# An encoder layer on one core: tokens t and n-t are added and subtracted ahead of the Fourier branch's channel product

## The chip, the cores and the metric

The kernel runs on one core of a Trainium2 chip. The metric is the device time of one execution in microseconds (us), as the median of the runs. The engines are TensorE (PE, its weight loads PEld), VectorE (DVE), ScalarE (ACT), GpSimd (POOL) and SyncE (SP), which issues nearly all DMAs of this kernel.

## What is computed

One layer is applied to two sequences with shared weights, the prompt of 512 tokens and the sample of 1024, 1024 channels each, all in float32. The part that the change touches is the Fourier branch of the mixer:

```python
h = rms_norm(x, g_pre_mix) * (1.0 + sc1) + sh1
u = h @ w_in                      # [xa | ya | xb | ga | gb]
xb = u[..., 2048:2560]
def fourier_mix(x):               # 4 groups of 128 channels
    xg = x.reshape(bsz, s, N_FNET_GROUPS, FNET_GROUP)
    f = jnp.fft.fft2(xg, axes=(1, 3), norm='ortho').real
    return f.reshape(bsz, s, D_FNET)
y_b = fourier_mix(xb) @ w_b_out
merged = sigmoid(ga) * y_a + sigmoid(gb) * y_b
```

Beside it run the RG-LRU branch (`xa`, with two scans in time, times a gelu gate `ya`), the gates `ga` and `gb`, the output projection, and a channel sub-layer with convolutions.

## The kernel before

Every float32 operand is split into two float32r parts, a rounded high part and a low part that is the difference; a product is three matmuls (high by high, high by low, low by high). Activations stand with channels on the partitions and tokens along the columns (`hb["hi"]`, `hb["lo"]`). The split of a weight tile is `prep_unit` / `split`: the high part on DVE (L110) or on ACT (L108), the low part always on DVE (L111).

The program is a list of steps, written out in order by `emit`. A step has a matmul part (`mm`), what follows it (`post`), and maybe a weight unit. Weight units are loaded through three raw buffers and split three steps ahead (`AHEAD`). What `defer` gets runs one or more steps later. Each engine carries out its instructions in the order in which `emit` writes them, and SP issues DMAs in that order too, waiting at each for the buffer that it fills or the tile that it stores. PSUM is a pool of four buffers of two banks (`ps`), SBUF tiles come from a pool of 40 buffers (`big`).

For each sequence the list runs: projections and LRU steps (`mix_heads`, `lru_step`), the Fourier product (`pq_steps`), the gate product (`ya_steps`), the DFT over tokens (`dft_steps`), then the merge. The last step ahead of `pq_steps` is in both sequences the last LRU step. It has four PSUM tiles of products, which ACT reads by tanh (L685), then ACT's exp, tanh and relu (L693 to L697); its DVE work is deferred in three parts: four multiply-adds (s1, L704 and L707), two square roots on ACT (s2, L711, with a table load), and multiplications, scans and a sum (s3, L716 to L724). So this work lies beside the first steps of `pq_steps`.

The channel part of the 2-D DFT is folded into the weights at the start (`fold_in`); the result goes to DRAM (`wxb`, 516 columns: 256 cosine, 4 for the middle frequency, 256 sine). `pq_steps` reads it back in units of 4 channel tiles by 258 columns. For the prompt it makes four token tiles by two halves of the columns; for the sample the later half of the tokens is kept back to front (`mirror`), the product is taken of both halves of the tokens, and the two are added (cosine) or subtracted (sine) behind the product, on DVE, out of PSUM. `dft_steps` then multiplies with cosine and sine tables over 512 token rows in both sequences, four tiles each; for the sample two edge products with the row of the middle token (`pq["row"]`, `odd`) are added for each of three outputs.

The lines of one product are these (the third pass wants the low part of the left operand):

```python
for q, (l, r) in enumerate(((lh, u.hi), (lh, u.lo), (ll, u.hi))):
    self.mmul(
        out, lhsT=l, rhs=r[:, w],
        start=(first and j == 0 and q == 0), stop=(last and j == nk - 1 and q == 2))
```

Of the kernel before, what the change touches and what calls it, by code (L numbers as in the profile page):

```python
# [10 lines left out]
F32 = mybir.dt.float32  # L11
F32R = mybir.dt.float32r
# [5 lines left out]
D = 1024  # L18
# [5 lines left out]
NPQ = 516  # L24
# [7 lines left out]
AHEAD = 3  # L32
LOAD_AHEAD = 5
# [16 lines left out]
class Seq:  # L50
    def __init__(self, name, idx, n, x, y):
        self.name, self.idx, self.n, self.x, self.y = name, idx, n, x, y
        self.nf = 1024 // n
        self.tt = n // 128
        self.chunks = n // 512
        self.groups = KT // self.nf
        self.mirror = n == 1024
        self.pq_tiles = self.tt // 2 if self.mirror else self.tt
# [13 lines left out]
class Enc:  # L72
# [40 lines left out]
    def split_all(self, pairs):  # L113
        """Splits out of PSUM: one engine's reads of a bank before the other's."""
# [112 lines left out]
    def fm_chunks(self, sq, ps, f, mirror=False):  # L227
        """Output columns and the operand's; a mirrored operand has the later half of the tokens back to front."""
        n = sq.n
        cols = [slice(0, 512), slice(n, n // 2, -1) if mirror else slice(512, 1024)]  # L230
        return [(ps[:, f, c * 512:(c + 1) * 512], cols[c]) for c in range(sq.chunks)]

    def fm_steps(self, sq, table, tiles, xh, xl, post, on_act=False, mirror=False):
        box = {}
        steps = []
        for f, m in enumerate(tiles):
            u = Unit(table[m], KT * 128, on_act=on_act)

            def mm(u=u, f=f):
                if f == 0:  # L240
                    box["ps"] = self.ps([128, sq.nf, sq.n])
                self.fm_mm(self.fm_chunks(sq, box["ps"], f, mirror), u, 0, xh(), xl())
# [6 lines left out]
    def setup(self):  # L249
        nc, a = self.nc, self.a  # L250
        self.wxb = self.dram([KT, 128, NPQ], "wxb")
        self.ident = self.const.tile([128, 128], F32, name="ident")
        self.fold = self.const.tile([128, 130], F32, name="fold")
# [67 lines left out]
    def ada_steps(self, job):  # L321
        """One part of the conditioning: a row of its weights per partition, two dot products with each."""
# [65 lines left out]
    def fold_in(self, tiles, out, ks):  # L388
        nc = self.nc
        for k in ks:  # L390
            ps = self.ps([128, 2, 512])
            v = ps[:, :, 0:260].rearrange("p h (g c) -> p h g c", g=2)
            for g in range(4):
                self.mmul(
                    v[:, g // 2, g % 2, :], lhsT=tiles[g][:, k * 128:(k + 1) * 128], rhs=self.fold,
# [3 lines left out]
                out=w[:, 0:256].rearrange("p (h g c) -> p h g c", h=2, g=2), in_=v[:, :, :, 0:64], func=AF.Copy)  # L399
            nc.scalar.activation(  # L400
                out=w[:, 260:516].rearrange("p (h g c) -> p h g c", h=2, g=2), in_=v[:, :, :, 64:128], func=AF.Copy)
            nc.vector.tensor_copy(
                w[:, 256:260].rearrange("p (h g c) -> p h g c", h=2, g=2), v[:, :, :, 128:129])
            out.append(w)

# [26 lines left out]
    def h_steps(self, sq, src, sub, box, quads=False):  # L432
# [15 lines left out]
        def tr(g):  # L448
            def f():
# [7 lines left out]
                mirror = sq.mirror and sub == 0  # L457
                w = n + 2 if mirror else n
                h = self.big([128, sq.nf, w], name="h")
                parts = [(slice(0, 512), slice(0, 512)), (slice(513, 1025), slice(1023, 511, -1))]  # L460
                for i in range(sq.nf):
                    k = g * sq.nf + i
                    for o, src in parts if mirror else [(slice(0, n), slice(0, n))]:
                        nc.scalar.activation(
                            out=h[:, i, o], in_=ps[:, i, src], func=AF.Identity,
                            scale=self.gs[:, sub, sq.idx, k:k + 1], bias=self.mod[:, 3 * sub, sq.idx, k:k + 1])
                if mirror:
# [1072 lines left out]
```

## Time and profile before

| | |
|---|---|
| median of 3 runs | 2117.44 us (2117.34 to 2117.49) |
| the profiled execution, first to last instruction | 2115.4 us |
| PE busy | 2096.1 us, 99% |
| DVE busy | 1424.4 us, 67% |
| ACT busy | 915.9 us, 43% |
| `pq_steps` of the prompt | 194.27 to 217.37 us |
| `pq_steps` of the sample | 692.61 to 738.66 us |

The profiled execution's own time is its span and what lies around it, 2.0 us below the median. Times in the rows further down are microseconds from the start of the span. A matmul's record is longer than the step from one matmul to the next, since matmuls overlap in the engine; so the cost of a matmul is read from a stretch of known count, not from its record. In rows in order of time the columns are: start, duration, engine, line, operation, output <- inputs, shapes, count, and in brackets the idle time ahead of it with what ended it; rows of several instructions are merged, and their duration runs from the first to the last.

### The profile page before, as it was taken

Reading aid. Unit: us, or ns where it says so; the run is one execution under the profiler, and the core shown is the slowest. Engines: PE = TensorE matmul, PEld = TensorE weight load, DVE = VectorE, ACT = ScalarE, POOL = GpSimd, SP = SyncE. Lnnn points to the kernel's source line nnn. Section 1 sums busy time; section 2 is a strip of 40 time slices with the busy share of each in tenths; the row PEclk is TensorE's granted clock in tenths of the full one; section 3 lists DMA queues with packets and bytes.
Section 4 is the critical chain, followed back from the end, with each engine's and each line's share of the span. In section 5 each row is a group of like instructions: output and inputs, shape, how many; then the busy total and the mean of one; then the engine's idle time right before and its main releaser. Section 6 shows DMA issues by size and latency. Waiting matters only on the chain.

```text
span 2115.4 us, 24826 instructions
## 1 busy us (share of the span) xinstructions
PE 2096.1 (99%) x9866; PEld 1721.6 (81%) x9866; DVE 1424.4 (67%) x1815; ACT 915.9 (43%) x1199; POOL 55.0 (3%) x124
## 2 busy tenths in 40 slices
PE   7999999999999999999999999999999999999998
PEld 6888888888888988888888888888888888888887
DVE  5787888667666734655676545649688887875553
ACT  2447355265464422144433335633344444455442
POOL 0000010000000000000100000000000000000000
PEclk9999999999999999999999999999999999999999
DMA  9343474332332413433453224332122222284422
GB/s 350 114 149 130 180 269 162 113 109 85 110 105 65 141 50 108 141 141 135 175 186 112 99 99 156 113 130 90 50 80 80 90 72 82 96 315 163 149 91 109
DMA packets 90803, 274.66 MB, mean 130 GB/s; under 512 B 8736, under 2 KB 26560, under 8 KB 90688
## 3 DMA queue, kind: packets, MB, share of 16 engines
q1 hardware_dynamic: 90688, 273.09, 37.1%
q8 instruction: 77, 1.26, 0.2%
q14 instruction: 38, 0.31, 0.1%
HBM read 234.22 MB, written 38.83 MB: 129 GB/s over the span
## 4 chain that ended last, share of the span: by engine, by line
PE 95%; ACT 2%; DVE 1%; DMA 1%; issue 0%; POOL 0%; SPq 0%; DVEq 0%; POOLq 0%; ACTq 0%
PE ps L200 94%; PE ps L203 1%; DMA x<-in_x_prompt_dram 0%; ACT xn L412 0%; ACT th L685 0%; DVE hl L111 0%; DMA x<-in_x_sample_dram 0%; DVE yb L964 0%; ACT th L695 0%; ACT ea L693 0%; POOL sm L430 0%; DVE th L716 0%; DVE th L721 0%; ACT xn L417 0%; DVE th L719 0%
## 5 line engine op out<-in xcount | busy, mean ns | idle before, releaser
L200 PE MATMUL ps<-hh,hl 128*128 128x512 f32 x2144 | 633.8, 395 | 0.0
L200 PEld LDWEIGHTS ps<-hh,hl 128*128 128x128 f32 x2144 | 403.7, 188 | 95.2 <-DVE hl L111 0.2
L200 PE MATMUL ps<-hl,ah 128*128 128x512 f32 x1440 | 452.2, 395 | 0.0
L200 PE MATMUL ps<-hl,hl 128*128 128x512 f32 (+1 forms) x1264 | 436.2, 378 | 0.0
L111 DVE TENSOR_TENSOR hl<-raw,hl 128x1024 fp32r<-128x1024 f32 (+2 forms) x244 | 293.8, 1206 | 163.3 <-ACT hl L108 160.9
L200 PE MATMUL ps<-hx,wq 128*128 128x512 f32 x1596 | 370.9, 394 | 0.0
L200 PEld LDWEIGHTS ps<-hx,wq 128*128 128x128 f32 x1596 | 299.6, 188 | 71.1 <-DVE wq L1222 0.2
L108 ACT ACTIVATE hl<-raw 128x1024 fp32r<-128x1024 f32 x196 | 205.6, 1054 | 270.8 <-PE ps L200 243.4
L200 PEld LDWEIGHTS ps<-hl,ah 128*128 128x128 f32 x1440 | 269.1, 188 | 61.5
L200 PE MATMUL ps<-hl,al 128*128 128x512 f32 x720 | 283.8, 394 | 0.0
L200 PEld LDWEIGHTS ps<-hl,hl 128*128 128x128 f32 x1264 | 238.3, 189 | 47.5
L200 PEld LDWEIGHTS ps<-hl,al 128*128 128x128 f32 x720 | 135.2, 188 | 31.8
L1318 DVE SCALAR_TENSOR_TENSOR cf<-ps,vec,cf 128x511 f32<-128x511 f32 (+1 forms) x100 | 75.2, 807 | 83.8 <-ACT cf L1310 83.6
L200 PE MATMUL ps<-yh,hl 128*128 128x512 f32 x384 | 111.9, 394 | 0.3 <-DVE hl L111 0.3
L1166 DVE SCALAR_TENSOR_TENSOR cf<-cq,vec,cf 128x1023 f32<-128x1023 f32 x76 | 97.0, 1277 | 0.0
L1221 ACT ACTIVATE wq<-wsum 128x512 fp32r<-128x512 f32 x76 | 46.1, 629 | 117.7 <-DVE wsum L1232 117.7
L200 PEld LDWEIGHTS ps<-yh,hl 128*128 128x128 f32 x384 | 71.5, 188 | 16.9 <-DVE hl L111 0.7
L1310 ACT ACTIVATE cf<-ps,vec 128x512 f32<-128x512 f32 (+1 forms) x50 | 39.1, 826 | 105.9 <-PE ps L200 105.9
L111 DVE TENSOR_TENSOR al<-fq,ah 128x512 fp32r<-128x512 f32 x88 | 57.3, 687 | 32.3 <-PE ps L200 18.4
L738 ACT ACTIVATE sg<-ps 128x1024 f32<-128x1024 f32 x24 | 24.7, 1028 | 118.8 <-PE ps L200 118.7
L200 PE MATMUL ps<-hl,hh 128*128 128x258 f32 x384 | 69.2, 282 | 0.0
L659 DVE SCALAR_TENSOR_TENSOR xc<-ps,vec,xc 128x511 f32<-128x511 f32 (+3 forms) x48 | 46.9, 1012 | 30.1 <-ACT xc L651 29.5
(181 smaller groups left out, 2359.6 us busy)
## 6 DMA issues: line engine op xcount, KB each, us to landing
raw<-in_w_up_dram SPq DMA_DIRECT2D x88, 512.0 KB, 3.5
raw<-in_w_down_dram SPq DMA_DIRECT2D x66, 512.0 KB, 3.5
ada<-in_w_adaT_dram SPq DMA_DIRECT2D x32, 512.0 KB, 4.7
raw<-in_w_o_dram SPq DMA_DIRECT2D x24, 512.0 KB, 3.5
fs<-cf SPq DMA_DIRECT2D x22, 512.0 KB, 2.6
fq<-fs SPq DMA_DIRECT2D x22, 512.0 KB, 5.8
ada<-in_w_ada_dram SPq DMA_DIRECT2D x16, 512.0 KB, 8.9
raw<-in_w_gb_dram SPq DMA_DIRECT2D x16, 512.0 KB, 4.3
```

The source lines that it names most:

```text
L108: nc.scalar.activation(out=hi, in_=src, func=AF.Copy)
L111: nc.vector.tensor_tensor(out=lo, in0=src[:, 0:keep], in1=hi[:, 0:keep].bitcast(F32), op=ALU.subtract)
L200: self.nc.tensor.matmul(*args, **kw)
L203: self.nc.tensor.transpose(*args)
L659: nc.vector.scalar_tensor_tensor(out=xc[:, f, o], in0=ps[:, f, o.start + d:o.stop + d], scalar=w[:, tap:tap + 1], in1=xc[:, f, o], op0=ALU ...
L738: self.nc.scalar.activation(out=t, in_=ps, func=AF.Tanh, scale=0.5)
L1166: nc.vector.scalar_tensor_tensor(out=box[key][:, o], in0=c[:, i], scalar=self.vec[:, V_FW + 3 * m + t:V_FW + 3 * m + t + 1], in1=box[key][ ...
L1221: nc.scalar.activation(out=hi, in_=src, func=AF.Copy)
L1310: nc.scalar.activation(out=acc[:, f, :], in_=ps[:, f, :], func=AF.Identity, scale=w[:, 1:2], bias=self.vec[:, V_FB + m:V_FB + m + 1])
L1318: nc.vector.scalar_tensor_tensor(out=acc[:, f, o], in0=ps[:, f, o.start + d:o.stop + d], scalar=w[:, tap:tap + 1], in1=acc[:, f, o], op0=A ...
```

## The change

The Fourier branch no longer multiplies tokens first and combines them afterwards. Where the modulated activations `h` are made, they are also stored to DRAM (`hrow`: four stores in the lead-in for the prompt, eight in `h_steps` for the sample). `pq_steps` is now four steps for each sequence, over two channel tiles each, with one unit of 2 x 512 columns (split with ACT for the high part). For each step the rows of its channel tiles are read back (`ld`, three steps ahead) and `pair_up` makes sum and difference of token t and token n-t and splits both (two steps ahead). The matmuls of all token tiles accumulate over the four steps: 260 columns with the sums (cosine), 252 with the differences (sine), and a one-row product for token n/2. For this `pq_steps` holds two PSUM buffers for the prompt, three for the sample. The prompt's DFT has two token tiles instead of four and the same edge products as the sample's. The mirrored copies, the additions behind the product, and the `mirror` arguments are gone. In the weights, the columns of the four groups are packed 63 by 63, with the edges in columns 252 to 259.

```diff
-NPQ = 516
+NPQ = 512
+NCOS = 260
+PAIR_AHEAD = 2
-        self.pq_tiles = self.tt // 2 if self.mirror else self.tt
+        self.pq_tiles = self.tt // 2
...
     def h_steps(...):
-                    for o, src in parts if mirror else [(slice(0, n), slice(0, n))]:
-                        nc.scalar.activation(out=h[:, i, o], in_=ps[:, i, src], func=AF.Identity, ...)
-                if mirror:
-                    nc.vector.tensor_copy(h[:, 0, 512:513], h[:, 0, 1024:1025])
+                    nc.scalar.activation(out=h[:, i, 0:n], in_=ps[:, i, :], func=AF.Identity, ...)
+                if sub == 0:
+                    self.defer(lambda: nc.sync.dma_start(
+                        out=self.hrow[sq.name][g * sq.nf:(g + 1) * sq.nf].rearrange("k p n -> p k n"), in_=h), 1)
...
     def lead_in(...):            # at the end of modulate
+            nc.sync.dma_start(
+                out=self.hrow[sq.name][k0 + i:k0 + i + nk].rearrange("k p n -> p k n"), in_=h)
...
+    def pair_up(self, sq, h, eo):
+        nc = self.nc
+        n, m = sq.n, sq.n // 2
+        for x in h:
+            nc.vector.tensor_copy(x[:, :, n:n + 1], x[:, :, m:m + 1])
+            t = self.big([128, sq.nf, 2, m], name="eo")
+            back = x[:, :, n:m:-1]
+            nc.vector.tensor_tensor(out=t[:, :, 0, :], in0=x[:, :, 0:m], in1=back, op=ALU.add)
+            nc.vector.tensor_tensor(out=t[:, :, 1, :], in0=x[:, :, 0:m], in1=back, op=ALU.subtract)
+            hi = self.big([128, sq.nf, 2, m], F32R, name="eh")
+            lo = self.big([128, sq.nf, 2, m], F32R, name="el")
+            self.split(hi, lo, t, act=True)
+            eo += [(hi[:, i], lo[:, i]) for i in range(sq.nf)]
...
     def pq_steps(...):
-        for t0 in range(0, sq.pq_tiles, per):
-            for half in range(2):
-                for k0 in range(0, KT, 4):
-                    src = self.wxb[k0:k0 + 4, :, half * HALF:(half + 1) * HALF].rearrange("k p c -> p k c")
-                    ...
-                        self.km_mm(outs, lhs, u, 4, HALF, k0 == 0, k0 == KT - 4)
+        for j in range(KT // 2):
+            u = Unit(self.wxb[2 * j:2 * j + 2].rearrange("k p c -> p k c"), 2 * NPQ, on_act=True)
+            def mm(u=u, j=j):
+                if j == 0:
+                    box["ps"] = [self.ps([128, 2, 512]) for _ in range(nt // 2 + 1)]
+                    ...
+                for i in range(2):
+                    ...
+                    for t in range(nt):
+                        for c, cols in enumerate(parts):
+                            for q, (l, r) in enumerate(((hi, wh), (hi, wl), (lo, wh))):
+                                self.mmul(box["out"][t][:, cols], lhsT=l[:, c, x], rhs=r[:, cols], ...)
+                    for q, (l, r) in enumerate(((hi, wh), (hi, wl), (lo, wh))):
+                        self.mmul(box["row"], lhsT=l[:, 1, 0:1], rhs=r[:, 0:NCOS], ...)
+            ...
+        for j in range(KT // 2):
+            st = (before + steps)[len(before) - PAIR_AHEAD + j]
+            st.post = self.both(st.post, pair(j))
+            st = (before + steps)[len(before) - PAIR_AHEAD - 1 + j]
+            st.post = self.both(st.post, ld(j))
...
     def dft_steps(...):
-        parts = (("cos", (0, 128, 132)), ("sin", (260, 388)))
+        parts = (("cos", ((0, 128), (128, 256), (132, 260))), ("sin", ((260, 388), (388, 512))))
-                    edge = sq.mirror and name == "cos"
+                    edge = name == "cos"
```

ScalarE around the prompt's last LRU step, before: `sg` is the eviction of the gate product ahead of it, `th_1627` to `th_1657` the four tanh evictions, `ea` and `th` behind them the exponentials, the `hl` and `pq` rows the splits of a weight unit and of the Fourier product.

```order
L738 ACTIVATE sg_1617<-ps_1562 128x1024
L685 ACTIVATE th_1627<-ps_1626,halfb 128x512 x2
L685 ACTIVATE th_1637<-ps_1636,halfb 128x512 x2
L685 ACTIVATE th_1647<-ps_1646,halfb 128x512 x2
L685 ACTIVATE th_1657<-ps_1656,halfb 128x512 x2
...
L697 ACTIVATE th_1647<-th_1647 128x1024
L711 ACT_TABLE_LOAD
L711 ACTIVATE th_1627<-th_1627 128x1024
L711 ACTIVATE th_1647<-th_1647 128x1024
L108 ACTIVATE hl_1747<-raw_1591 128x1024
L117 ACTIVATE pq_1800<-ps_1688 128x258
```

And now: `eh` is the rounded copy of a pair's sums and differences (`eo`).

```order
L736 ACTIVATE sg_1625<-ps_1568 128x1024
L109 ACTIVATE eh_1631<-eo_1628 128x1024
L109 ACTIVATE hl_1639<-raw_1535 128x1024
L683 ACTIVATE th_1645<-ps_1644,halfb 128x512 x2
L683 ACTIVATE th_1655<-ps_1654,halfb 128x512 x2
...
L695 ACTIVATE th_1665<-th_1665 128x1024
L109 ACTIVATE eh_1700<-eo_1697 128x1024
L109 ACTIVATE hl_1711<-raw_1566 128x1024
L109 ACTIVATE eh_1752<-eo_1749 128x1024
L709 ACT_TABLE_LOAD
L709 ACTIVATE th_1645<-th_1645 128x1024
L709 ACTIVATE th_1665<-th_1665 128x1024
```

The first pair's copy and a weight copy have come between the eviction of the gate product and the tanh evictions, and the second and third pair's copies stand behind the LRU step's last relu and ahead of the table load for its square roots.

VectorE behind the same step, before: the splits of four weight units are ahead of the LRU step's multiply-adds (`th` <- `th`, `xc`).

```order
L111 TENSOR_TENSOR hl_1526<-raw_1391,hl_1526 128x1024
L110 CAST hl_1557<-raw_1422 128x1032
L111 TENSOR_TENSOR hl_1557<-raw_1422,hl_1557 128x1032
L110 CAST hl_1588<-raw_1490 128x1032
L111 TENSOR_TENSOR hl_1588<-raw_1490,hl_1588 128x1032
L110 CAST hl_1621<-raw_1529 128x1032
L111 TENSOR_TENSOR hl_1621<-raw_1529,hl_1621 128x1032
L704 SCALAR_TENSOR_TENSOR th_1637<-th_1637,xc_1345 128x1024
L704 SCALAR_TENSOR_TENSOR th_1657<-th_1657,xc_1345 128x1024
L707 SCALAR_TENSOR_TENSOR th_1637<-ea_1666,th_1637 128x1024
L707 SCALAR_TENSOR_TENSOR th_1657<-ea_1672,th_1657 128x1024
```

And now, from the first pair on (`hr` are the rows read back, `el` the low parts):

```order
L112 TENSOR_TENSOR el_1632<-eo_1628,eh_1631 128x1024
L112 TENSOR_TENSOR hl_1639<-raw_1535,hl_1639 128x1024
...
L803 TENSOR_TENSOR eo_1697<-hr_1635 128x2x256
L804 TENSOR_TENSOR eo_1697<-hr_1635 128x2x256
L112 TENSOR_TENSOR el_1701<-eo_1697,eh_1700 128x1024
L702 SCALAR_TENSOR_TENSOR th_1655<-th_1655,xc_1351 128x1024
L702 SCALAR_TENSOR_TENSOR th_1675<-th_1675,xc_1351 128x1024
L705 SCALAR_TENSOR_TENSOR th_1655<-ea_1684,th_1655 128x1024
L705 SCALAR_TENSOR_TENSOR th_1675<-ea_1690,th_1675 128x1024
L112 TENSOR_TENSOR hl_1711<-raw_1566,hl_1711 128x1024
L800 COPY hr_1704<-hr_1704 128x2
L803 TENSOR_TENSOR eo_1749<-hr_1704 128x2x256
```

The multiply-adds now stand behind the low part of the second pair, which waits for ScalarE's copy of it; the next pair's sums stand behind the multiply-adds and one weight split.

SyncE ahead of the prompt's Fourier product, before:

```order
L123 DMA raw_1490<-wxb 128x4x258
L123 DMA raw_1529<-wxb 128x4x258
L123 DMA raw_1560<-wxb 128x4x258
L739 DMA sgp_71<-sg_1555 128x1024
L123 DMA raw_1591<-in_w_ya_dram 128x1024
L329 DMA ada_1619<-in_w_adaT_dram 128x1024
```

And now:

```order
L124 DMA raw_1496<-wxb 128x2x512
L124 DMA raw_1535<-wxb 128x2x512
L124 DMA raw_1566<-wxb 128x2x512
L832 DMA hr_1593<-hrowp 128x2x512
L737 DMA sgp_71<-sg_1561 128x1024
L124 DMA raw_1599<-in_w_ya_dram 128x1024
L832 DMA hr_1635<-hrowp 128x2x512
```

The row reads (`hr`) have come in behind the weight loads, which wait for a raw buffer.

## Rows read from the trace of the kernel before

**Rows 1.** The page's first part: busy us, share of the span, instructions.

```profile
PE 2096.1 (99%) x9866; PEld 1721.6 (81%) x9866; DVE 1424.4 (67%) x1815; ACT 915.9 (43%) x1199; POOL 55.0 (3%) x124
```

**Rows 2.** TensorE's waits: line, waited for: us in total, times, longest us.

```profile
PE ps L200 <- DVE hl L111: 1.1, 4, 0.5
```

**Rows 3.** Windows over both `pq_steps`: stretch, length, engines' busy (count), clock, DMA, GB/s.

```profile
194.27:217.37 23.10, 23.10 (x194) 23.10 (x192) 17.82 (x20) 17.43 (x25) 0.00 (x0) 1.00 0.40 148
...
692.61:738.66 46.05, 46.05 (x385) 46.05 (x384) 35.22 (x50) 18.93 (x26) 0.00 (x0) 1.00 0.44 155
```

**Rows 4.** One tile's instructions, ns min/median/max: a difference of 512 columns on VectorE.

```profile
L1124 DVE TENSOR_TENSOR tq<-hq x4: 682/684/686, 1433.0 to 1480.4; 128x512 f32<-128x512 f32 x4
```

**Rows 5.** ScalarE in order of time, the prompt's last two LRU steps.

```profile
163.25 4.73 ACT L685 ACTIVATE th<-ps,halfb 128x512 f32<-128x512 f32 x8
...
195.62 0.81 ACT L693 ACTIVATE ea<-th,nk 128x512 f32<-128x512 f32 x1
...
204.16 1.28 ACT L711 ACT_TABLE_LOAD   x1
205.46 2.01 ACT L711 ACTIVATE th<-th 128x1024 f32<-128x1024 f32 x2
207.37 1.04 ACT L108 ACTIVATE hl<-raw 128x1024 fp32r<-128x1024 f32 x1
```

**Rows 6.** VectorE in order of time, the prompt's last LRU step; last row the sample's.

```profile
187.78 1.23 DVE L111 TENSOR_TENSOR hl<-raw,hl 128x1024 fp32r<-128x1024 f32 x1
...
194.72 2.35 DVE L704 SCALAR_TENSOR_TENSOR th<-th,xc 128x1024 f32<-128x1024 f32 x2
...
206.55 1.23 DVE L716 TENSOR_TENSOR th<-th,th 128x1024 f32<-128x1024 f32 x1 [1.22 <-ACT th L711]
207.81 2.34 DVE L719 TENSOR_TENSOR_SCAN th<-ea,th 128x512 f32<-128x512 f32 x2
210.06 1.20 DVE L716 TENSOR_TENSOR th<-th,th 128x1024 f32<-128x1024 f32 x1
...
686.48 1.22 DVE L724 TENSOR_TENSOR th<-th,th 128x1024 f32<-128x1024 f32 x1
```

**Rows 7.** SyncE's loads of folded weights, in order; landing of loads, 150:230.

```profile
177.59 13.68 SPq L123 DMA_DIRECT2D raw<-wxb  x3
...
DMA to landing us min/median/max: 3.4/4.5/6.2
```

**Rows 8.** ScalarE in order of time, the sample's last LRU step.

```profile
692.81 1.12 ACT L685 ACTIVATE th<-ps,halfb 128x1024 f32<-128x1024 f32 x1 [0.28 <-PE ps L200]
693.82 1.23 ACT L693 ACTIVATE ea<-th,nk 128x1024 f32<-128x1024 f32 x1
...
700.96 1.28 ACT L711 ACT_TABLE_LOAD   x1
```

**Rows 9.** Windows in the lead-in, columns as in rows 3 (clock third from last).

```profile
24.00:26.00 2.00, 0.30 (x1) 0.14 (x1) 1.29 (x8) 1.14 (x2) 0.00 (x0) 1.00 1.10 375
...
28.00:30.00 2.00, 2.00 (x6) 1.27 (x6) 1.93 (x5) 0.00 (x0) 0.00 (x0) 0.50 1.10 348
30.00:32.00 2.00, 2.00 (x27) 1.46 (x29) 1.95 (x4) 0.00 (x0) 0.00 (x0) 0.90 1.10 348
```

**Rows 10.** Lead-in in order of time on SyncE, ScalarE, TensorE; landing of conditioning loads.

```profile
33.69 5.06 SPq L505 DMA_DIRECT2D ada<-in_w_ada_dram  x4
...
37.39 1.46 ACT L583 ACTIVATE h<-ps,mod,gs 128x512 f32<-128x512 f32 x2 [11.08 <-PE ps L203]
...
54.28 1.96 PE L200 MATMUL ps<-ada,cact 128*32 128x128 f32 x64
...
DMA to landing us min/median/max: 8.2/8.6/9.0
```

**Rows 11.** TensorE: a narrowest float32r group by form; the fold in order of time.

```profile
L200 PE MATMUL ps<-hl,pq 128*128 128x258 f32 x180 | 22.4, 284 | 0.0
...
10.34 8.42 PE L200 MATMUL ps<-fold,wxbt 128*128 128x130 f32 x58 [0.48 <-DMA wxbt<-in_wxbT_dram]
```

More of the change, by code (lines that the diff above doesn't have):

```diff
@@ L225, in km_mm, with fm_chunks, fm_steps @@
                         start=(first and j == 0 and q == 0), stop=(last and j == nk - 1 and q == 2))
[L227 to L233, printed above, removed]
+    def fm_chunks(self, sq, ps, f):
+        cols = [slice(c * 512, (c + 1) * 512) for c in range(sq.chunks)]
+        return [(ps[:, f, c], c) for c in cols]
+    def fm_steps(self, sq, table, tiles, xh, xl, post, on_act=False):
         box = {}
@@ L250, in setup @@
         nc, a = self.nc, self.a
+        self.hrow = {q.name: self.dram([KT, 128, q.n], "hrow" + q.name) for q in (self.p, self.s)}
         self.wxb = self.dram([KT, 128, NPQ], "wxb")
         self.ident = self.const.tile([128, 128], F32, name="ident")
-        self.fold = self.const.tile([128, 130], F32, name="fold")
+        self.fold = self.const.tile([128, 128], F32, name="fold")
         self.vec = self.const.tile([128, V_END], F32, name="vec")
@@ new lines, in pq_steps, with ld, f @@
+        n, nt = sq.n, sq.pq_tiles
+        box, eo = {}, []
+        parts = (slice(0, NCOS), slice(NCOS, NPQ))
+        rows = {}
+        def ld(j):
+            def f():
+                rows[j] = []
+                for i in range(2 // sq.nf):
+                    k = 2 * j + i
+                    x = self.big([128, sq.nf, n + 2], name="hr")
+                    nc.sync.dma_start(
+                        out=x[:, :, 0:n], in_=self.hrow[sq.name][k:k + sq.nf].rearrange("k p n -> p k n"))
+                    rows[j].append(x)
+            return f
@@ L893, in post @@
                             nc.scalar.activation(out=z["edge"][r:r + 32, at], in_=e, func=AF.Copy)
-                    self.split_all([(z[name, o][:, :, at], box["ps"][0][:, o, 0:HALF]) for o in range(2)])
+                    rows = [slice(0, b - a) for a, b in cols]
+                    self.split_all([(z[name, o][rows[o], :, at], box["ps"][0][rows[o], o, 0:HALF]) for o in range(2)])
                     if len(cols) == 3:
@@ L1395, in mix @@
             out = heads
-            out += e.pq_steps(q, h1[q.name], pq[q.name])
+            out += e.pq_steps(q, pq[q.name], heads)
             out += e.ya_steps(q, h1[q.name], hs[q.name], yb[q.name])
@@ L1435, in _dft @@
     k = np.arange(n // 2 + 1)
-    rows = n // 2 if n == 1024 else n
+    rows = n // 2
     m = np.arange(rows)
@@ L1443, in _dft @@
         w[:, :n // 2 + 1] = fn(ang)
-        if fn is np.cos and rows < n:
+        if fn is np.cos:
             w[0, 1::2] = 0.0
```

147 lines of the change are left out of this document (64 added, 83 removed).

## The prediction

> **What bounds the kernel now.** I read the busy shares first, then what TensorE waited for, then the two stretches that the change rewrites, then the queues of ScalarE (ACT) and VectorE (DVE) around them. TensorE has a matmul in flight for 2096.1 us of the 2115.4 us span [rows 1]. Its waits after the start are a few tenths of a microsecond; the largest that a split causes is in the list for L111, 1.1 us in four pieces [rows 2]. So a matmul taken away is worth its full step, and a wait put in front of TensorE costs its full length, because nothing later is idle to absorb it. The profiled span stands 2.0 us below the median of the runs, 2117.4 us; I sum on the span and carry those 2.0 us along.
>
> The stretch that the change rewrites is the product with the folded Fourier weights, `pq_steps`: 194.27 to 217.37 us for the prompt, 692.61 to 738.66 us for the sample, clock 1.00 and TensorE busy throughout [rows 3]. By the code these are 192 and 384 matmuls, which gives 23.10/192 = 0.1203 us and 46.05/384 = 0.1199 us a step; I use 0.1203.
>
> **What is removed.** The new stage has 8 x 2 x 2 x 3 + 8 x 3 = 120 matmuls for the prompt and 8 x 4 x 2 x 3 + 24 = 216 for the sample (the 24 are the one-row products for the token in the middle). That is 72 and 168 fewer. The prompt's DFT over tokens needs two tiles instead of four: 60 become 36, with 6 edge products counted. Together 264 matmuls x 0.1203 = 31.8 us off TensorE. I price all new forms, 252 and 260 columns and one-row weights, like 258 columns; the bound is with the rivals. The Trainium skill, page "TensorE: Matmul & The Clock Gate", section "Back-to-back issue gap", gives N/2.4 + 2.5 ns for one step, 110 ns at 258 columns by its formula. By that the removed matmuls would be an estimated 29 us; the measured 0.1203 us decides.
>
> **What is added: the pairs.** Each of the four steps q0 to q3 now needs its own operand: rows read back from DRAM, a copy of one column, an add and a subtract on DVE, a rounding copy on ACT, a subtract for the low part on DVE. The prices: add and subtract of 512 columns 0.68 us each [rows 4], 1.35 with the copy; the ACT copy 1.04 (L108) [rows 5]; the low part 1.15 from start to start, 1.23 alone [rows 6]. One round is 1.35 + 1.05 + 1.2 = 3.6 us, one after the other, since DVE's next instruction stands behind the low part and that behind ACT. The prompt has one round a step, the sample two (7.2 us), while a step of TensorE lasts 30 x 0.1203 = 3.6 and 54 x 0.1203 = 6.5 us. That alone would nearly balance. It doesn't, because the rounds stand in the queues of the last LRU step, and the order shows where: ahead of its tanh (pair 0), behind its exp/tanh/relu (pair 1), and with its scans between pairs 2 and 3. I walk both queues with the durations of before.
>
> **Prompt.** DVE ends the LRU weights' low part at 188.95 [rows 6], then those of q0 and q1: 190.1 and 191.2. The row load for pair 0 stands in SP's queue behind the weight load of q3, which waits for q0's low part (as the third load of that row did in before, out at 191.3 [rows 7]): out at 190.6. A load there lands in 3.4 to 6.2 us, median 4.5 [rows 7], so 195.1. Add and subtract to 196.45, ACT copy to 197.5, low part 198.7. The LRU's eight tanh, 0.59 us each [rows 5], stand behind this copy and one weight copy, so they start at 198.5 and not while the LRU's products run. q0 writes the PSUM buffer that the first two free: 199.7. TensorE's LRU products end at 194.27, so it is idle 5.4 us; q0 ends at 203.3. ACT: tanh to 203.25, then exp, tanh and relu, ten instructions, 195.62 to 204.16 or 8.5 us [rows 5], to 211.75; only then pair 1's copy, 212.8, low part 214.0. Of each three passes the third wants the low part, so q1 runs as from 213.75: idle 10.4 us, end 217.35. DVE next has four multiply-adds at 1.15 (L704) [rows 6] to 218.6, q3's low part 219.75, pair 2: 221.1, 222.15, 223.3. q2 as from 223.05: idle 5.7, end 226.65. ACT loads its table (1.28) and takes a root (1.0) [rows 5] to 224.45; DVE multiplies, scans twice, multiplies, scans twice, adds, 1.25 + 2.25 + 1.2 + 2.3 + 1.15 (the first half is in [rows 6], the second like it), to 232.6, then one low part 233.75 and pair 3: 235.1, 236.15, 237.3. q3 as from 237.05: idle 10.4, end 240.65. Before it ended at 217.37: **23.3 us later**.
>
> **Sample.** DVE is free of the earlier scans at 687.6 [rows 6]; its weights are rounded earlier and no load is late. Low part of q1 688.75; pair 0's rounds end at 692.35 and 695.95. ACT then has a weight copy to 695.8 and the LRU's four tanh at 1.0 [rows 8]; q0 starts at 696.8 where before it started at 692.61 (idle 4.2) and ends at 703.3. Tanh to 699.85, exp to relu 693.82 to 700.96 or 7.1 us [rows 8], to 706.95; pair 1's rounds 709.2 and 712.8; q1 from 708.95 to 715.8 (idle 6.0, the second round's 0.35 with it). DVE 4.6 + 1.15, pair 2's rounds 722.15 and 725.75; q2 to 728.75 (6.4). Root 726.85, scans and sums 8.1, low part, pair 3's rounds 739.7 and 743.3; q3 to 746.3 (11.0). Before it ended at 738.66: **7.6 us later**, although 168 matmuls, 20.2 us, are gone.
>
> So waits of 31.9 and 27.7 us stand against 31.8 us removed. Net: 23.3 + 7.6 - 2.9 (prompt's DFT) = +28.0 us.
>
> **The clock after a wait.** At 24 to 26 us TensorE was busy 0.30 of 2 us; in 28 to 30 us its granted clock was 0.50, the level of 1.2 GHz, and 0.90 in the next 2 us [rows 9]. TensorE would be wholly idle for 4 to 11 us ahead of each step here, so I expect the 1.2 GHz level behind these waits too. A step of 0.1203 can then at most double. In q0 to q2 the next wait swallows it; only q3 pays, at most 3.6 us in each sequence; about half, 3 us in all, is taken, 0 and 7 are the bounds. The Trainium skill, same page, section "What's actually happening", says that the throttled clock is the default and activity releases it; by that rule the sum is +31 us, without it +28, and the row at 28 us agrees with it.
>
> **At nothing.** Four stores of the modulated rows enter the lead-in on SP. The second waits for ACT to 38.85 us, so the last four conditioning loads leave some 5 us after 33.69 [rows 10]; the last of them goes out near 44 and with 8.6 us lands near 53, and its first reader is at 54.28 [rows 10]. Cover 1 us; bound 0 to 2 us. The sample's eight stores and the pairs' loads are 0.5 MB each where queues have room (DMA share 0.40 and 0.44 [rows 3]). Evictions after q3 lie beside the first product of `ya_steps`, which has its own PSUM buffer. ACT takes the weights' rounding from DVE in these steps; that is in the walk. Merge and sample DFT keep their counts.
>
> Forecast: 2115.4 + 28 + 3 + 2.0 = **2148 us**. By its own bounds (clock 0 to 7, lead-in 0 to 2, the first load 1.1 early or 1.7 late, 4 us for the walk) 2139 to 2160.
>
> **Rivals.**
> *The pairs are ready in time.* DVE is busy 17.82 of 23.10 us and ACT 17.43 in the prompt's stretch, 35.22 and 18.93 of 46.05 in the sample's [rows 3]: by busy shares alone there is room, and less work on ACT's side is asked for than it idles in the sample. If the queues' order did not bind (pair 1's copy is offered to ACT at 201 us and only its place holds it until 211.75), the waits would go and 31.8 us would stay: 2085.6 us, faster. It decides at 28 us: with that much less of the 59.6 us of waits walked, it is a gain. Against it: both queues run in order throughout these rows, and each pair's wait is behind instructions with a duration. Chance 0.09, including smaller gains; 0.06 that waits and saving cancel within 0.2% (about what a measurement of this kernel can tell from no change).
> *Moving operands under 258 columns are slow.* No float32r matmul of before has fewer (the least is in [rows 11]); half of the new ones have 252. Upper bound: the plain float32 fold, 58 records in 8.42 us [rows 11], two records for each product of 130 columns, 2.2 ns a column, so 0.56 us for 252 columns, 0.44 more. In the prompt only q3's twelve count, 5.3 us; in the sample a step becomes 17.1 us and TensorE the bound, 18.9 us more: 2172 us. Lower bound: nothing. I take nothing, since 258 columns lies next to 252. Chance 0.13, with 2156 to 2172.
> *The walk is right and something I cost at nothing isn't* (lead-in, a load): 0.05, 2160 to 2175.
> *The forecast:* 0.67.
>
> **How the numbers follow.** Slower 0.67 + 0.13 + 0.05 = 0.85, same 0.06, faster 0.09. The range leaves out the faster and equal cases and the far end of the others: 2135 to 2172, which holds the forecast's 0.67 and most of the 0.18 above it.
>
> **What would show it.** Right: TensorE's waits in the list name the ACT copy and the DVE low part of the pairs, four gaps in each sequence, near 5, 10, 6, 10 us and 4, 6, 6, 11 us; between them matmuls at 0.12 us; the granted clock under 1.00 in both stretches only; the prompt's DFT 24 matmuls shorter. Wrong: q1 starting less than 5 us after q0's end (the queues did not hold it), steps of more than 0.2 us at full clock for 252 columns, or waits of TensorE before 60 us on conditioning loads.

## The result, and the profile after

| | before | after |
|---|---|---|
| median of the runs | 2117.47 us (4 runs, 2117.34 to 2117.82) | 2152.83 us (4 runs, 2152.57 to 2154.59) |
| profiled execution, first to last instruction | 2115.4 us | 2152.8 us |
| `pq_steps` of the prompt | 23.10 us | 52.28 us |
| `pq_steps` of the sample | 46.05 us | 56.72 us |

The changed kernel is slower: 1.0168 times the time before, 95% interval 1.0154 to 1.0182, or 35.4 us. Forecast were 2148 us, range 2135 to 2172. The profiled execution after is the longest of its four (2154.59 us); so spans differ by 37.4 us, 2 us more than the medians do.

The first part of the page after (busy us, share of the span, instructions), to be read against [rows 1], and the granted clock in 40 slices of the span:

```profile
PE 2086.5 (97%) x9602; PEld 1704.4 (79%) x9602; DVE 1433.5 (67%) x1816; ACT 928.4 (43%) x1195; POOL 54.5 (3%) x124
...
PEclk9998799999999889999999999999999999999999
```

TensorE has 264 instructions fewer, but its busy time falls by 9.6 us only, and DVE and ACT are about as busy as before: over the whole span no engine has become the bound by its amount of work. What is new is in TensorE's list of waits (line, waited for: us in total, times, longest us), where [rows 2] had nothing of more than a few tenths from these stages:

```profile
PE ps L201 <- ACT eh L109: 30.4, 6, 8.9
PE ps L201 <- ACT th L683: 12.9, 2, 8.5
...
PE ps L201 <- DVE el L112: 3.3, 6, 0.8
```

These are 46.6 us, in two stretches: 25.4 in the prompt's, 21.3 in the sample's. Windows over the two (columns as in [rows 3], which they answer: stretch, length, busy us of PE, PEld, DVE, ACT and POOL, clock, DMA, GB/s):

```profile
195.54:247.82 52.28, 26.86 (x121) 23.36 (x121) 28.96 (x32) 25.11 (x31) 0.00 (x0) 0.64 0.42 143
719.41:776.13 56.72, 35.49 (x216) 32.87 (x217) 36.76 (x42) 27.45 (x28) 0.00 (x0) 0.73 0.35 117
```

In the prompt 120 matmuls take 26.86 us, 0.224 us each, where 0.12 were counted; the clock column says why: 0.64 of full speed in the prompt and 0.73 in the sample, as means over work and waits. TensorE in order of time, the prompt's four steps; in brackets the idle time ahead and what ended it:

```profile
204.05 0.80 PE L201 MATMUL ps<-hl,eh 128*128 128x260 f32 x2 [8.51 <-ACT th L683]
...
216.84 0.80 PE L201 MATMUL ps<-hl,eh 128*128 128x260 f32 x2 [6.34 <-ACT eh L109]
218.10 0.58 PE L201 MATMUL ps<-hl,el 128*128 128x260 f32 x1 [0.46 <-DVE el L112]
...
226.28 0.51 PE L201 MATMUL ps<-hl,eh 128*128 128x260 f32 x2 [2.16 <-ACT eh L109]
227.54 0.58 PE L201 MATMUL ps<-hl,el 128*128 128x260 f32 x1 [0.76 <-DVE el L112]
...
240.66 0.80 PE L201 MATMUL ps<-hl,eh 128*128 128x260 f32 x2 [6.74 <-ACT eh L109]
```

And the sample's four:

```profile
723.79 0.80 PE L201 MATMUL ps<-hl,eh 128*128 128x260 f32 x2 [4.38 <-ACT th L683]
...
734.75 0.50 PE L201 MATMUL ps<-hl,eh 128*128 128x260 f32 x2 [2.09 <-ACT eh L109]
736.00 0.59 PE L201 MATMUL ps<-hl,el 128*128 128x260 f32 x1 [0.76 <-DVE el L112]
...
747.91 0.80 PE L201 MATMUL ps<-hl,eh 128*128 128x260 f32 x2 [4.17 <-ACT eh L109]
...
766.05 0.80 PE L201 MATMUL ps<-hl,eh 128*128 128x260 f32 x2 [8.93 <-ACT eh L109]
```

Each step waits for the same things: a PSUM buffer that the LRU's tanh evictions hold (q0), then the pair's copy on ACT, then its low part on DVE. ACT's queue over the same time (start, duration) shows what the copies stood behind:

```profile
200.84 1.06 ACT L109 ACTIVATE eh<-eo 128x1024 fp32r<-128x1024 f32 x1 [10.48 <-DVE eo L804]
201.80 1.04 ACT L109 ACTIVATE hl<-raw 128x1024 fp32r<-128x1024 f32 x1
202.75 4.72 ACT L683 ACTIVATE th<-ps,halfb 128x512 f32<-128x512 f32 x8
...
214.78 1.06 ACT L695 ACTIVATE th<-th 128x1024 f32<-128x1024 f32 x1
215.75 1.04 ACT L109 ACTIVATE eh<-eo 128x1024 fp32r<-128x1024 f32 x1
```

The first copy holds the tanh evictions back until 202.75; the second pair's sums are ready at 205.7 and its copy starts at 215.75, without a gap behind the LRU's last relu. On DVE, the first row says that the rows from DRAM came late, the last ones that the fourth pair stands behind multiply-adds and scans:

```profile
199.31 0.17 DVE L800 COPY hr<-hr 128x2 f32<-128x2 f32 x1 [6.92 <-DMA hr<-hrowp]
...
216.82 1.23 DVE L112 TENSOR_TENSOR el<-eo,eh 128x1024 fp32r<-128x1024 f32 x1 [11.12 <-ACT eh L109]
217.96 2.35 DVE L702 SCALAR_TENSOR_TENSOR th<-th,xc 128x1024 f32<-128x1024 f32 x2
...
233.38 2.34 DVE L719 TENSOR_TENSOR_SCAN th<-ea,th 128x512 f32<-128x512 f32 x2
235.75 1.23 DVE L722 TENSOR_TENSOR th<-th,th 128x1024 f32<-128x1024 f32 x1
236.89 1.22 DVE L112 TENSOR_TENSOR hl<-raw,hl 128x1024 fp32r<-128x1024 f32 x1
238.03 0.16 DVE L800 COPY hr<-hr 128x2 f32<-128x2 f32 x1
```

### The profile page after: what moved, and what is told of

It reads as the page before. It is cut to its first block, busy times and chain, and to the rows that moved or that the text cites. A ratio compares the mean times of both kernels' runs of the same rounds, so it can differ in the third digit from the quotient of the medians.

```text
span 2152.8 us, 24316 instructions
## 1 busy us (share of the span) xinstructions
PE 2086.5 (97%) x9602; PEld 1704.4 (79%) x9602; DVE 1433.5 (67%) x1816; ACT 928.4 (43%) x1195; POOL 54.5 (3%) x124
## 4 chain that ended last, share of the span: by engine, by line
PE 90%; DVE 4%; ACT 3%; issue 1%; DMA 1%; POOL 0%; SPq 0%; DVEq 0%; POOLq 0%; ACTq 0%
PE ps L201 89%; PE ps L204 1%; ACT th L683 1%; DVE hl L112 0%; DVE th L714 0%; DVE th L719 0%; ACT th L693 0%; DVE el L112 0%; ACT eh L109 0%; ACT ea L691 0%; DMA hr<-hrowp 0%; DVE th L717 0%; DMA wxbt<-in_wxbT_dram 0%; DVE eo L804 0%; ACT xn L412 0%
## 5 line engine op out<-in xcount | busy, mean ns | idle before, releaser
L112 DVE TENSOR_TENSOR hl<-raw,hl 128x1024 fp32r<-128x1024 f32 (+2 forms) x240 | 287.3, 1200 | 163.9 <-ACT hl L109 161.4
L201 PE MATMUL ps<-hl,hl 128*128 128x512 f32 x1072 | 380.7, 394 | 0.0
L109 ACT ACTIVATE hl<-raw 128x1024 fp32r<-128x1024 f32 x204 | 213.6, 1053 | 265.6 <-PE ps L201 238.5
L201 PEld LDWEIGHTS ps<-hl,hl 128*128 128x128 f32 x1072 | 201.3, 188 | 47.2
L201 PE MATMUL ps<-hl,eh 128*128 128x260 f32 (+2 forms) x224 | 58.7, 363 | 43.3 <-ACT eh L109 30.4
L201 PEld LDWEIGHTS ps<-hl,eh 128*128 128x128 f32 (+1 forms) x224 | 46.5, 250 | 47.7 <-ACT eh L109 32.5
```

Source lines behind the costliest of these rows:

```text
L109: nc.scalar.activation(out=hi, in_=src, func=AF.Copy)
L112: nc.vector.tensor_tensor(out=lo, in0=src[:, 0:keep], in1=hi[:, 0:keep].bitcast(F32), op=ALU.subtract)
L201: self.nc.tensor.matmul(*args, **kw)
```

## The experiments

The theory: the loss is the order in two in-order queues, in which the pairs share ACT and DVE with the last LRU step, and the slow clock behind the waits. Rivals: the work is simply too much for ACT and DVE; the 252-column matmuls are slow; the clock is low for another reason. All edits are on the changed kernel.

**The saving alone (saving_alone).** No pairs; the products take the unpaired activations:

```diff
-                    hi, lo = eo.pop(0)
+                    hi, lo = (hb[v][k].rearrange("p (c m) -> p c m", c=2) for v in ("hi", "lo"))
...
-        for j in range(KT // 2):
-            st = (before + steps)[len(before) - PAIR_AHEAD + j]
-            st.post = self.both(st.post, pair(j))
...
```

> The changed kernel without its pairs: no rows are read back, no sums and differences are made, and the Fourier products take the first and second halves of the unpaired activations as left operands (so the Fourier branch doesn't compute the reference's values). Every matmul of the change stays, the stores of the rows too. Theory (the loss is all waits on the pairs behind the LRU work in ACT's and DVE's queues): no wait of TensorE in either stretch, clock 1.00 there, steps of 0.12 us with 252 and 260 columns; 264 matmuls fewer are worth 31.8 us, the sample's projections some 2 to 3 us more, the lead-in costs 1.2: about 2084 us. Rival (252-column float32r operands are slow): no waits, but steps of up to 0.56 us at full clock in half of the matmuls, 2090 to 2135 us.

Measured: 2096.94 us, 0.9902 (0.9882 to 0.9922) of before, which took 2117.84 us beside it. It is 13 us more than the theory gave, and not for the rival's reason. Windows of this kernel, a part of the prompt's stretch without waits and the sample's whole product:

```profile
203.00:206.00 3.00, 3.00 (x27) 2.61 (x25) 0.89 (x1) 2.90 (x5) 0.00 (x0) 1.00 0.00 0
...
693.20:719.00 25.80, 25.80 (x219) 24.92 (x218) 16.91 (x14) 16.57 (x18) 0.00 (x0) 1.00 0.38 137
```

Those 216 matmuls of 260, 252 and 260 columns take 25.8 us, 0.1194 us each: the rival of slow 252 columns falls. In the sample nothing waits, and its 20.2 us are gained in full. In the prompt TensorE waits without any pair:

```profile
208.01 0.38 PE L201 MATMUL ps<-hl,hh 128*128 128x260 f32 x1 [1.92 <-ACT hl L109]
209.27 0.58 PE L201 MATMUL ps<-hl,hh 128*128 128x260 f32 x1 [0.88 <-DVE hl L112]
219.90 1.22 PE L201 MATMUL ps<-hh,hl 128*128 128x512 f32 x2 [3.74 <-DVE hl L112]
```

These are weights. The rounding of q3's unit, now on ACT, stands behind the LRU's relu; the low parts for `ya_steps` stand behind its scans. With the slow clock behind them (0.50 from 210 to 214 us) they take back the prompt's saving: the sample's first conv eviction comes at 392.92 us, at 390.26 in the kernel before. I read this as the loss of cover: the matmuls taken away had hidden the LRU step's own queue. No run parts it from the other difference, that the change rounds these weights on ACT and the kernel before on DVE. Either way, even with free pairs the change would have been worth 20.9 us and not 31.8.

**The copy on DVE (hi_on_dve).**

```diff
-            self.split(hi, lo, t, act=True)
+            self.split(hi, lo, t)
```

> The changed kernel with the rounded copy of the pairs on DVE instead of ACT (0.72 us more on DVE a round, 1.05 less on ACT). Theory (two in-order queues are coupled by the copy): pair 0 no longer holds the tanh evictions, pair 1 no longer stands behind exp, tanh and relu; in the prompt the waits ahead of q0 and q1 shrink to about 6 and under 2 us, in the sample to about 1 and under 1, while those ahead of q2 and q3 stay at 4 to 9 us because the multiply-adds and scans are DVE's own: about 13 us less in each sequence, 2127 us, 2120 to 2135. Rival (DVE is the bound by its amount of work): nothing gained or a loss, 2150 us or more.

Measured: 2126.75 us (4 runs, 2125.72 to 2127.79), as the theory had it (of the single waits only the prompt's at q2, 2.7 us, is under the 4 expected). The waits for ACT are gone but 0.8 us; DVE's own order is left:

```profile
PE ps L201 <- DVE eh L111: 25.7, 5, 6.7
...
PE ps L201 <- ACT th L683: 0.8, 1, 0.8
```

More work on the busier engine made the kernel 26 us faster. Ahead of q0 to q3 the prompt waits 6.7, 0, 2.7 and 5.5 us, the sample 0.8, 0, 4.6 and 6.2. So most of the lost time came from the coupling of the two queues through the copy, not from DVE's amount of work. ACT has less to do in this kernel; that its amount of work wasn't the cause either is for the next run to show, which takes nothing off it.

**The LRU behind the Fourier steps (lru_late).** `s0` are the last LRU step's exp, tanh and relu:

```diff
...
         def post():
+            if late:
+                self.defer(lambda: s0((0, 1)), 4)
+                self.defer(s1, 4)
+                self.defer(s2, 5)
+                self.defer(s3, 6)
+                return
+            s0((0, 1))
             self.defer(s1, 0)
```

> The changed kernel with one difference: of the last LRU step of each sequence only the tanh evictions stay in place; its exp, tanh, relu and multiply-adds go behind the step q3, the roots one step later, the scans two. No work is left out. Theory (order in the queues): the waits ahead of q1, q2 and q3 (16.9 us in the prompt, 16.9 in the sample) go; the wait ahead of q0 stays (8.5 and 4.4 us), and the slow clock behind it is now paid in q0 instead of q3: 2152.8 - 33.8 = about 2119 us, 2115 to 2124. Rival (ACT and DVE simply can't do the pairs in the time of the matmuls, whatever the order): most of the waits stay, 2140 us or more.

Measured: 2124.91 us (6 runs), ratio to before 1.0035 (1.0022 to 1.0048); 28 us less than the changed kernel, not the 34 expected, and just outside the 2115 to 2124 given. The waits ahead of q1 to q3 are down from 33.8 to 5.9 us, and those ahead of q0 stay. Both rows are of TensorE's list, of this kernel:

```profile
PE ps L201 <- ACT th L683: 12.3, 2, 7.9
...
PE ps L201 <- ACT eh L109: 3.4, 3, 1.9
```

On the profiled spans the two stretches are 25.4 and 15.1 us shorter, more than the waits alone, since their slow clock goes too. But from the end of the prompt's Fourier steps to the start of the sample's it takes 10.7 us longer. There the LRU's work now meets the conditioning products and fills DVE (54.34 of 60 us busy from 240 to 300 us): TensorE waits 6.3 us in all in pieces of under 1 us, mostly for weights, and its granted clock is 0.95 in these 60 us. So the order was most of the loss, and work put off was partly paid later.

**The gate product last (gate_last).** One line sets that the last gate product comes behind the last LRU step (`'ps'` are the names of the two sequences, so it holds for both):

```diff
-        jobs += fill[:1] + [sq.groups - 1] + fill[1:]
+        jobs += [sq.groups - 1] + fill if sq.name in 'ps' else fill[:1] + [sq.groups - 1] + fill[1:]
```

> The changed kernel with one line different: the last gate product of each sequence (11 us of matmuls) comes behind the last LRU step instead of ahead of it, so that ACT and DVE have that long for the LRU's exp to relu, roots and scans before the Fourier product starts. Nothing is left out or added. Theory (order in the queues): the waits of each sequence fall by about the 11 us and some clock time with them, 24 to 28 us in all: 2125 to 2129 us. Rival (amount of work on ACT and DVE): the gate product brings its own evictions and weights, the waits stay: 2145 us or more.

Measured: 2131.46 us (2130.26 and 2132.66): 21.4 us less than the changed kernel, short of the 24 to 28 expected and far from the rival's 2145. Waits in the two stretches are 15.7 and 17.7 us, in the changed kernel 25.4 and 21.3. What is left is the same mechanism a step on: ACT's copy for the second pair waits for sums that stand behind the LRU's scans on DVE:

```profile
215.56 1.06 ACT L109 ACTIVATE eh<-eo 128x1024 fp32r<-128x1024 f32 x1 [6.72 <-DVE eo L804]
```

**The rows earlier (rows_early).**

```diff
-            st = (before + steps)[len(before) - PAIR_AHEAD - 1 + j]
+            st = (before + steps)[len(before) - PAIR_AHEAD - 2 + j]
```

> The changed kernel with the rows read back one step earlier (two steps before their sums instead of one). Nothing is left out. Theory (the prompt's first pair waits for its rows, which leave SP at 191.7 us and land at 199.3): DVE makes the first sums at about 193 us, the tanh evictions follow 6 us earlier and the whole stretch of the prompt ends some 6 us earlier; the sample, where no pair waits for rows, stays: about 2147 us. Rival (the rows were not what is late; the loads, which wait for buffers, now hold back others in SP's queue): 2152 us or more.

Measured: 2153.47 us (2151.91 and 2155.03): no gain, so the rival's number. But the trace shows both halves of it. DVE in this kernel, the prompt's first pair and the sample's second:

```profile
195.92 0.17 DVE L800 COPY hr<-hr 128x2 f32<-128x2 f32 x1 [3.27 <-DMA hr<-hrowp]
...
728.94 0.69 DVE L803 TENSOR_TENSOR eo<-hr 128x512 f32<-128x512 f32 x1 [8.65 <-PE ps L201]
```

The rows land 3.4 us earlier, and the prompt's stretch ends at 244.54 instead of 247.82 us. They leave SP at 190.83, only 0.9 us earlier than the 191.69 of the changed kernel, since a weight load stands ahead of them until 190.41; as the rival has it, the queue limits what an earlier place brings. In the sample the second pair's sums wait 8.65 us, 5.1 in the changed kernel, for a buffer that a matmul still reads, and the stretch takes 61.9 instead of 56.7 us. One more row buffer is taken there from the same 40 SBUF buffers, which fits: an earlier load paid for with memory. No run changed the number of buffers.

**TensorE kept busy (keep_warm).** Matmuls that nobody reads stand in the place of q3's wait:

```diff
...
+                if j == 3:
+                    t = self.ps([128, 2, 512])
+                    x = hb["hi"][0]
+                    count = 50 if n == 512 else 68
+                    for r in range(count):
+                        self.mmul(t[:, 0, 0:HALF], lhsT=x[:, 0:128], rhs=x[:, 0:HALF], start=r == 0, stop=r == count - 1)
```

> The changed kernel with extra matmuls ahead of q3 that nobody reads: 50 of 258 columns in the prompt, 68 in the sample, 6.0 and 8.2 us by 0.12 us each, in the place of waits of 6.7 and 8.9 us. Theory (the clock is at the 1.2 GHz level in q3 because TensorE stood idle ahead of it): the granted clock stays at 1.00 through q3, its steps take 0.12 us instead of 0.21, and q3 is 3.3 us shorter in each sequence although TensorE does more: 2152.8 - 6.6 = about 2146 us. Rival (the low clock comes from something else in these stretches, not from the idle time): nothing gained, or the extra matmuls run over: 2152 to 2156 us.

Measured: 2150.77 us (2149.12 and 2152.42), between the two. The clock did what the theory says. First the changed kernel in a window of q3, then this kernel in q3 of the prompt:

```profile
240.60:244.00 3.40, 2.88 (x11) 2.58 (x12) 3.36 (x3) 1.91 (x3) 0.00 (x0) 0.50 0.53 211
```

```profile
241.00:243.00 2.00, 1.72 (x14) 1.62 (x15) 2.00 (x3) 0.87 (x1) 0.00 (x0) 1.00 0.35 143
243.00:245.00 2.00, 2.00 (x18) 1.85 (x17) 0.49 (x1) 0.46 (x1) 0.00 (x0) 1.00 0.75 209
```

q3 takes 4.68 us instead of 7.16 in the prompt and 7.95 instead of 10.08 in the sample, 4.6 us together; at full speed it waits up to 0.6 us longer for the low parts. So the idle time is what lowered the clock, shown by the trace; of the size in the median only 2 us are seen, and the runs of both kernels scatter by as much.

**Reading back to front (reversed_half, reversed_odd).** Between the two stretches the changed kernel gains 1.1 us that no term of mine had. From one conv eviction of the sample to the next are 39.21 us before, 38.97 after, with the same matmuls. Rows of before, then of after:

```profile
491.09 1.21 ACT L651 ACTIVATE xc<-ps,vec 128x1024 f32<-128x1024 f32 x1 [7.71 <-PE ps L200]
530.31 1.21 ACT L651 ACTIVATE xc<-ps,vec 128x1024 f32<-128x1024 f32 x1 [7.71 <-PE ps L200]
```

```profile
519.04 1.21 ACT L649 ACTIVATE xc<-ps,vec 128x1024 f32<-128x1024 f32 x1 [7.54 <-PE ps L201]
557.99 1.21 ACT L649 ACTIVATE xc<-ps,vec 128x1024 f32<-128x1024 f32 x1 [7.54 <-PE ps L201]
```

The kernel before reads the later half of the tokens from column 1024 down to 513. First the direction alone was put back, then the layout with it:

```diff
+        ins = [cols[0], slice(1023, 511, -1)] if back else cols
```

> The changed kernel with one difference: in the sample's projections and gate products the second half of the moving operand is read back to front (columns 1023 down to 512), as the kernel before does (so the sample's later tokens come out in another order than the reference's). From one group's conv eviction to the next in the sample are 39.2 us in the kernel before and 38.96 in the changed one, with the same matmuls. Theory A (the reading back to front costs some 3.5 ns a matmul): the distance goes back to 39.2 us and the time rises by 2 to 3 us, to about 2155.5. Theory B (the difference comes from elsewhere, as the layout of the tiles): 38.96 us stays, 2152.8.

```diff
+        ins = [cols[0], slice(1024, 512, -1)] if back else cols
...
+                wide = n + 2 if odd else n
```

> The changed kernel with the sample's activations laid out as in the kernel before: tiles 1026 columns wide, the later half at columns 513 to 1024, read from column 1024 back to 513 by the projections and gate products (the values then stand in another order than the reference's). From one conv eviction to the next are 38.96 us in the changed kernel, 39.09 with columns 1023 to 512 read back to front, 39.21 in the kernel before. Theory A (the odd start of the half costs the other half of the difference): 39.21 us here, some 1 us more in all than with columns 1023 to 512. Theory B (something else in the kernel before): 39.09 us.

Measured: 39.09 us a group with the direction alone (mean of five), 39.24 with the layout as well, 39.21 in the kernel before. Both theories of the first run look half right. Each figure is of one execution, though, and the eight kernels here that read forward lie between 38.88 (rows_early) and 39.00 us (lru_late). So it is shown that the reading of the kernel before, direction and layout together, costs 0.2 to 0.4 us a group, 3 to 5 ns for each of the 72 matmuls that read this half. How it divides is an estimate: 0.13 us or 1.8 ns for the direction, 0.15 us or 2.1 ns for the layout, each hardly more than the spread of 0.12 us. In the times (2152.76 and 2156.21 us) so little can't be told from scatter.

**All of it together (pairs_ahead).** gate_last, with the last LRU step's work put off as in lru_late, the copy on DVE, more lead for the prompt's pairs and rows, and the conditioning products spread out:

```diff
+LRU_LATE = {'p': (6, 6, 7, 8), 's': (5, 5, 6, 7)}
...
-        jobs += fill[:1] + [sq.groups - 1] + fill[1:]
+        jobs += [sq.groups - 1] + fill if sq.name in 'ps' else fill[:1] + [sq.groups - 1] + fill[1:]
...
-            self.split(hi, lo, t, act=True)
+            self.split(hi, lo, t, act=sq.name not in 'ps')
...
-            st = (before + steps)[len(before) - PAIR_AHEAD + j]
+            st = (before + steps)[len(before) - {'p': 3, 's': 2}[sq.name] + j]
...
-            st = (before + steps)[len(before) - PAIR_AHEAD - 1 + j]
+            st = (before + steps)[len(before) - {'p': 3, 's': 2}[sq.name] - {'p': 2, 's': 1}[sq.name] + j]
...
-        steps = place(steps, side, [ya - 10] + [ya + i // 2 for i in range(16)] + [ya + 10] + [ya + 22] * 9)
+        steps = place(steps, side, [ya - 10] + [ya + i for i in range(16)] + [ya + 16] + [ya + 22] * 9)
```

> All that the runs so far point to, put together; nothing is left out: the last gate product behind the last LRU step, that step's work behind its tanh evictions put off until after q3, the pairs' rounded copy on DVE, the prompt's pairs made three steps ahead and its rows read two steps before that, and the prompt's conditioning products (which fill DVE in the gate product after it) one a step instead of two. Theory: waits of 1 us each are left in front of the Fourier steps, some 10 us remain where DVE is full in the prompt up to 300 us; 264 matmuls fewer (31.8 us) and the sample's 1.6 us faster projections against 1.2 in the lead-in, some 16 us of waits and a few of slow clock: 2100 to 2110 us, faster than both. Rival (the pairs cost more than the matmuls, however they are placed): 2117 us or more.

Measured: 2103.04 us (4 runs, 2102.14 to 2104.05), 0.9929 (0.9912 to 0.9945) of before, which took 2118.05 us beside it: with all of its arithmetic the change is faster than both, by another order and by one copy on another engine. The kernel before was not run in this order; its waits for weights are 1.1 us in all [rows 2], so these had little left to gain there. In the prompt's Fourier steps and in the sample's the clock is 1.00 and 0.7 and 1.9 us of waits are left. Windows inside the two stretches:

```profile
200.00:206.00 6.00, 6.00 (x53) 5.69 (x52) 5.86 (x10) 1.81 (x2) 0.00 (x0) 1.00 0.83 315
...
713.00:720.00 7.00, 6.03 (x47) 5.17 (x46) 6.62 (x11) 1.06 (x1) 0.00 (x0) 1.00 0.49 154
```

The largest part of what is missing up to the full saving lies between 270 and 300 us: 7.8 us of waits for DVE (the largest 3.0 and 2.8, for the merge's sum and the conditioning's last product) and a granted clock of 0.77, where the kernel before has no wait and 1.00. DVE is busy 28.93 of these 30 us, so here its amount of work is the limit. That the prompt gains nothing shows in the sample's first conv eviction, which comes behind the prompt's part; first the kernel before, then this one:

```profile
390.26 1.21 ACT L651 ACTIVATE xc<-ps,vec 128x1024 f32<-128x1024 f32 x1 [8.82 <-PE ps L200]
```

```profile
394.11 1.21 ACT L650 ACTIVATE xc<-ps,vec 128x1024 f32<-128x1024 f32 x1 [8.70 <-PE ps L202]
```

Up to there the kernel is 3.9 us later than before (0.9 of it from the lead-in), although 96 matmuls of the prompt are gone; from there to the end it is 17.0 us shorter. The whole gain comes with the sample's product. A kernel that makes the pairs for the sample alone, with the prompt left as it was, was not run.

## Why the prediction was right

It named the mechanism, the place and the sign, and the median came 4.8 us above the forecast. Term by term, on the profiled spans (37.4 us):

| stretch, by TensorE's marks | forecast | measured |
|---|---|---|
| up to the prompt's product | 0 | +1.3 |
| `pq_steps` of the prompt | +23.3, and half of the clock's 3 | +29.2 |
| DFT of the prompt | -2.9 | -2.6 |
| from there to the sample's product | 0 | -1.1 |
| `pq_steps` of the sample | +7.6, and half of the clock's 3 | +10.7 |
| behind it | 0 | -0.1 |

- **The walk of the two queues** held. From q0's start to the first low part of q1 it had 14.3 us, measured 14.05 (204.05 to 218.10); from there to q2's 9.3, measured 9.4 (to 227.54); to q3's 14.0, measured 14.4 (to 241.92).
- **The waits** were walked as 31.9 and 27.7 us and are 25.4 and 21.3. The difference is nearly all the slow clock in q0 to q2, whose longer steps eat into the next wait, as the prediction said; the ends of the stretches don't move by it. So single waits are far from those walked: ahead of the prompt's q2 2.2 and 0.8 us instead of 5.7. One of the signs named for being wrong even came, q1 less than 5 us behind q0's end: 2.1 us in the sample. The queues held there all the same, since from q0's start to q1's first low part it is 12.2 us (723.79 to 736.00), walked 12.4; the sign had left out that a slow q0 ends later.
- **The clock** was the term of the wrong size: 3 us taken, 0 to 7 bounded. q3 runs at 0.50 for the prompt's whole step, 6.7 us of work instead of 3.6, and for the first half of the sample's and more, 9.6 us instead of 6.5: 3.1 and 3.1 us. I had assumed that the level comes back within half of a step. By the Trainium skill's rule (page "TensorE: Matmul & The Clock Gate", section "What's actually happening") activity has to release the throttle; the traces agree, with 0.50 behind waits of 2.1 to 8.9 us and 1.00 where matmuls filled the wait.
- **The first rows** were the second: "lands in 3.4 to 6.2 us, median 4.5". They left SP at 191.69 and were there at 199.31, 7.6 us, with weight loads, a second row load and a store in the same microseconds; the second row load took 9.9 us, and the prompt's four 6.6 in the median. So the median of the rows before was too short here. Against the end of the LRU's products that is 2.9 us more than walked, and all of the prompt's stretch slid by it: 23.3 + 2.9 + 3.1 = 29.3.
- **At nothing**: the lead-in's stores were. The 1.3 us stand there in this execution, but the first LRU product starts between 82.3 and 83.9 us in ten kernels with this same lead-in, and at 82.3 before. Not costed, and not nothing, was the reading back to front that the change removes: seven groups by 0.24 us are 1.7 us, of which 1.1 are left in the table.
- **The rivals.** Slow 252 columns: refuted by 0.1194 us a step. Pairs ready in time: it would not have given the 2085.6 us that I wrote, but 2097 (saving_alone). I took every removed matmul as gain as soon as the pairs don't wait, and left out what the LRU's own queue and the weights behind it cost once those matmuls are gone. The forecast was not touched by it, since the walk followed the real queues; a rival's price was.

## What to carry to other kernels

Before work is moved from behind a product to ahead of it, write down where it lands in each in-order queue and what stands ahead of it there; busy shares of 77% and less said "room" here, and the queues brought 47 us of waits. A removed matmul can be worth less than its time, as when something used it as cover: here 20.9 of 31.8 us even without the pairs. When a change loses by order, the order can be changed back: the same arithmetic, placed anew, went from 35 us slower to 15 us faster. And look at each stretch by itself: here the sample gained all of it and the prompt nothing.

## What was not expected of the hardware

- A moving operand of 512 float32r columns costs 3 to 5 ns more when it lies at columns 513 to 1024 of its tile and is read back to front: 39.21 and 39.24 us against 38.88 to 39.00 for 72 such matmuls among a group's others. About half of it seems to be the direction (39.09 us in one execution).
- Behind an idle time of only 2.2 us TensorE ran at the 1.2 GHz level for almost a whole step (q2 of the prompt, clock 0.57 over the 7.9 us from 226.0). The step ahead of it had been slow too (0.53), but that isn't needed. In the sample q0 had come back to 1.00, and behind 2.09 and 0.76 us of waiting the clock fell again (0.50 from 736.0 to 738.6 us); in saving_alone it fell from 1.00 to 0.50 behind 1.92 and 0.88 us. The sample's q0 and q1 in windows (columns as above):

```profile
730.00:732.70 2.70, 2.65 (x23) 2.27 (x21) 0.67 (x2) 2.64 (x4) 0.00 (x0) 1.00 0.00 0
...
734.70:737.00 2.30, 1.50 (x6) 1.30 (x7) 2.24 (x4) 0.00 (x0) 0.00 (x0) 0.68 0.25 100
```

- In the lead-in of kernels that are the same up to there, the moment at which the clock falls differs (0.50 in 28 to 30 us in some executions, in 30 to 32 in others), and 1.6 us of time with it. Differences of that size between two single executions say nothing.
